# Where a weight tile begins: weights that meet 256 columns start 192 bytes into a tile 256 bytes longer

## The chip, the cores and the metric

The kernel runs on one core of one Trainium2 chip. The metric is the device time of one execution in microseconds. Three runs of the kernel before gave 2215.52, 2216.24 and 2218.65 us, a median of 2216.24.

## What is computed

A decoder trunk of two layers over 512 tokens of width 1024, in float32, batch 1. Each layer is: half a SwiGLU feed-forward block, a token mixer (retention in layer 0, forgetting attention in layer 1), half a SwiGLU again, and a gate that adds a projected per-layer input. Each has an RMSNorm ahead of it.

```python
def swiglu(x, w_in, w_out):
    g, u = jnp.split(x @ w_in, 2, axis=-1)
    return (jax.nn.silu(g) * u) @ w_out

for i in range(DEPTH):
    h = h + 0.5 * swiglu(rmsnorm(h, nw[0]), ffn_w_in[i, 0], ffn_w_out[i, 0])
    hn = rmsnorm(h, nw[1])
    h = h + (retention(hn, ...) if i % 2 == 0 else forgetting_attention(hn, ...))
    h = h + 0.5 * swiglu(rmsnorm(h, nw[2]), ffn_w_in[i, 1], ffn_w_out[i, 1])
    gate = jax.nn.sigmoid(rmsnorm(h, nw[3]) @ ple_w_gate[i])
    h = h + gate * (p[i] @ ple_w_proj[i])
```

The four feed-forward blocks (FFNs) have 2816 hidden columns each.

## The kernel before

**Products.** The activations stay in SBUF with the features on the partitions and the 512 tokens along the row. To keep float32 accuracy every operand is split into a high half (a rounding to the matmul's type, `fp32r`) and a low half (the rest), and a product is made as three: high by high, high by low, low by high. `mm3` (L311) does that with 512 columns of tokens, one moving operand of 128x512 each. The weights are the stationary operand, 128x128 a piece.

**The FFN's first matrix.** Each FFN has 22 column blocks of 128 hidden columns (gate and up). Two of them, the plain ones (`plain`, L511), are made in the ordinary way from products of 256 columns (L524): 8 steps over the width, two halves of the tokens, gate and up, three products each, 192 per FFN. The other 20 go through a scheme that saves products: the 2 by 2 blocks of the weights and of the activations are added up, and seven block products stand for eight (`start`, `one`, `two`, `three`, from L530). Each of the seven is a call of `product` (L490), whose matmuls are all on L493: 12 matmuls of 128x256, with the weight's high half 8 times and its low half 4. Of the seven, two take the block as it is loaded (`pair.t`, a tile that the profile calls `w`), four take sums of blocks (`pair.s`, tiles `s12` and `s34`, in the profile `s`), one takes the block `pair.x` (tile `a12`, in the profile `a`). So 84 products of 256 columns stand for a column block, 24 with `w`, 48 with `s`, 12 with `a`, and 4 x 20 x 84 = 6720 for all FFNs.

**Order in an FFN.** The hidden columns are worked in three chunks, (0, 6), (6, 14) and (14, 22), the first of which holds the two plain blocks. At the end of a chunk the next block is begun, and then `out_blocks` multiplies the chunk by the second matrix with `mm3`, 512 columns, from `w` tiles. So the 256-column stretch of the second and third chunk starts behind 512-column products. In the first chunk `two` copies a bank to SBUF with ScalarE (L545), behind the gating of the plain blocks, and `three` waits for it.

**Weights.** `Weights` holds a plan of all weight pieces in the order of their use. A piece (4 KB of each partition's row) is loaded from HBM into a `wraw` tile on SyncE's queue, ScalarE rounds it into the high half of a tile (L82, L121), and the low half is made by a subtraction on VectorE or GpSimd (L83), or by a negation and a transfer that adds the piece once more (L122, GpSimd's queue). `take` asks for two pieces beyond the one it returns. The high and low half lie one behind the other in a tile of 2 x 1024 floats, 8192 bytes of a row. Three such tiles rotate in the pool `wpool`. The last gating layer (`ple` with two parts of 256 tokens each) uses its last seven pieces for both parts: five in a pool `wkept` of the same kind of tile, two in `unit_b` tiles that are free by then. That layer's `mm3` products have 256 columns.

**Places.** The program puts its tiles one behind the other in each partition's row. Taken modulo 256 bytes, the activation tiles (`unit_a` to `unit_d`) begin at byte 32, and so does every 128x128 piece of the three rotating `w` tiles. Behind `wpool` lie the temporary tiles and the statistics, and then what a stage opens for itself: the FFN's `s12`, `s34` and `a12` tiles, or the five kept tiles, all of which begin at byte 224. The turned probabilities of the attention (`thi`, `tlo`) begin at byte 96. A step of a piece (512 bytes), of a half of the tokens (1024) or from the high to the low half does not change this remainder.

Of the kernel before, what the change touches and what calls it, by code (L numbers as in the profile page):

```python
# [12 lines left out]
F32R = mybir.dt.float32r  # L13
# [4 lines left out]
P = 128  # L18
# [17 lines left out]
class Pair:  # L36
# [3 lines left out]
    def __init__(self, ffn, q, r):  # L40
        self.ffn, self.q, self.r, self.direct = ffn, q, r, False
# [13 lines left out]
class Weights:  # L55
# [3 lines left out]
    def __init__(self, tc, raw_pool, pool):  # L59
        self.tc, self.nc, self.raw_pool, self.pool = tc, tc.nc, raw_pool, pool  # L60
        self.plan, self.ready, self.used = [], [], 0
        self.low = self.nc.vector
        self.limit, self.spare = None, []
        self.sum_pool, self.open_ffn, self.pairs_used = None, None, 0
        self.ahead, self.behind = 0, ()

    def emit(self, upto):
        while len(self.ready) < min(upto, self.limit):
            src = self.plan[len(self.ready)]
            self.ready.append(self.first(src) if isinstance(src, Pair) else self.chunk(src))  # L70
            self.emit_sums()

    def load(self, src):
        raw = self.raw_pool.tile([P, 1024], F32, name="wraw")
        self.nc.sync.dma_start(out=raw[:, : src.shape[1]], in_=src)
        return raw

    def split(self, raw, hi, lo, src=None):
        if self.low is None and src is not None:
            self.negated(raw, hi, lo, src)  # L80
            return
        self.nc.scalar.copy(hi, raw)  # L82
        self.low.tensor_tensor(out=lo, in0=raw, in1=hi.bitcast(F32), op=ALU.subtract)  # L83

    def chunk(self, src):
        n = src.shape[1]
        raw = self.load(src)
        if self.spare:
            tiles = [self.spare.pop(0)() for _ in range(4)]
            for i in range(2):  # L90
                self.split(raw[:, 512 * i : 512 * (i + 1)], tiles[i], tiles[2 + i])
            return Halves(tiles[0:2]), Halves(tiles[2:4])
        t = self.pool.tile([P, 2, 1024], F32R, name="w8")
        self.split(raw[:, :n], t[:, 0, :n], t[:, 1, :n], src)
        return t[:, 0, :], t[:, 1, :]

    def emit_parts(self, parts):

        nc = self.nc
        halves = lambda ap: ap.rearrange("p (h c) -> p h c", h=2)  # L100
        tiles = [
            (
                self.raw_pool.tile([P, 1024], F32, name="wraw"),
                self.pool.tile([P, 2, 1024], F32R, name="w8"),
            )
            for _ in range(2)
        ]
        for j0, j1 in parts:
            cs = slice(j0 * P, j1 * P)
            for src, (raw, t) in zip(self.plan, tiles):  # L110
                r, hi, lo = (halves(x)[:, :, cs] for x in (raw, t[:, 0, :], t[:, 1, :]))
                nc.sync.dma_start(out=r, in_=halves(src)[:, :, cs])
                nc.vector.tensor_copy(hi, r)
                nc.vector.tensor_tensor(out=lo, in0=r, in1=hi.bitcast(F32), op=ALU.subtract)
            yield
        self.ready += [(t[:, 0, :], t[:, 1, :]) for _, t in tiles]
# [7 lines left out]
    def first(self, pair):  # L124

        pair.raw = self.load(pair.q)
        pair.t = self.pool.tile([P, 2, 1024], F32R, name="w8")
        hi, lo = pair.t[:, 0, :], pair.t[:, 1, :]
        if pair.direct:
            self.split(pair.raw, hi, lo)  # L130
        else:
            self.negated(pair.raw, hi, lo, pair.q)
# [55 lines left out]
def trunk(ctx, tc, a):  # L188
# [16 lines left out]
    W = Weights(tc, wraw, wpool)  # L205
# [5 lines left out]
    ffn_src = []  # L211
    for i in range(4):
        ins = [Pair(i, a["ffn_w_in"][i, m, 0], a["ffn_w_in"][i, m, 1]) for m in range(NF)]
# [12 lines left out]
    ple_g = [[a["ple_gate"][l, m] for m in range(KB)] for l in range(2)]  # L226
    ple_p = [[a["ple_proj"][l, c] for c in range(2)] for l in range(2)]
# [11 lines left out]
    def plan_ple(l):  # L239
        W.plan += [ple_p[l][0]] + ple_g[l][0:5] + [ple_p[l][1]] + ple_g[l][5:8]  # L240
# [22 lines left out]
    plan_ffn(3)  # L263
    plan_ple(1)
    W.limit = len(W.plan) - KEPT


    hall = hpool.tile([P, KB, S], F32, name="hall")
# [42 lines left out]
    def mm3(out, wh, wl, xh, xl, first, last):  # L311
        nc.tensor.matmul(out, wh, xh, start=first, stop=False)  # L312
        nc.tensor.matmul(out, wh, xl, start=False, stop=False)  # L313
        nc.tensor.matmul(out, wl, xh, start=False, stop=last)  # L314
# [877 lines left out]
    norms[2].extra = ud  # L1192
    first = W.emit_parts(((0, 1), (1, 2), (2, 4)))
    next(first)
    load_x(1, 2)
    load_x(2, 4)
# [15 lines left out]
    def ffn_ple(i, l, n, mid, nxt, stack, apool, parts):  # L1212
        phi, plo = [], []

        def load():
            pv = a["pT"][l].rearrange("(b p) t -> b p t", p=P)
            for b in range(2):
                t1 = temp()
                nc.sync.dma_start(out=t1, in_=pv[b])
                phi.append(unit(uc))  # L1220
                plo.append(unit(uc))
                split(t1, phi[b], plo[b])

        ffn(i, n, mid, stack, apool, load)
        stack = open_ffn(i + 1) if i < 3 else None
        ple(l, mid, nxt, phi, plo, parts)
        return stack
# [101 lines left out]
```

## Time and profile before

| | before |
|---|---|
| median of three runs | 2216.24 us |
| the profiled execution | 2215.98 us |
| its span, first to last instruction | 2214.2 us |
| mean granted TensorE clock | 0.99 |
| TensorE matmuls | 13525 |
| VectorE, ScalarE, GpSimd busy | 66%, 54%, 21% |
| bytes read from HBM | 262.71 MB |

The profile is that of one execution. Times are in microseconds from the start of the span, and `ns` where it is said. PE is TensorE multiplying, PEld is TensorE loading weights, which overlaps with it, DVE is VectorE, ACT ScalarE, POOL GpSimd. A row names the line of the kernel, the engine, the operation, the tile that is written and those that are read (buffer numbers left out), and the shape. Matmuls overlap, so that the duration of one says less than the distance from the start of one to the start of the next. The timeline joins neighbours with the same line and tiles and gives the start of the group, its length and the count.

### The profile page before, as it was taken

To read this page: it belongs to the slowest core of one execution; us is meant where nothing else is said; L and a number is where in the kernel's file an instruction comes from. 1 tells how busy PE (TensorE), PEld (TensorE's weight loads), DVE (VectorE), ACT (ScalarE), POOL (GpSimd) and SP (SyncE) were. 2 spreads that over 40 slices of the span, in tenths; PEclk is the share of its full clock that TensorE was granted. 3 is DMA by queue.
4 is the path that set the end of the run, shared out by engine and by line. 5 is a ranking of instruction groups with operands and counts; after the bars stand their busy time and mean duration, and the time that the engine had idled before them with its cause. 6 is when DMAs were issued, how large, how long until landed. Compare 5 with 4: busy or idle time off the path is not lost.

```text
span 2214.2 us, 34442 instructions
## 1 busy us (share of the span) xinstructions
PE 2148.7 (97%) x13525; PEld 1933.3 (87%) x13525; DVE 1459.4 (66%) x2631; ACT 1203.1 (54%) x2027; POOL 466.8 (21%) x352
## 2 busy tenths in 40 slices
PE   7999999999999999999998999999999999999997
PEld 7999997888888798989887989898788898999987
DVE  8687776352533677867758677675575686777764
ACT  7565453343333564746545646364786775554643
POOL 0011013444344000101142001012243200110154
PEclk9999999999999999999999999999999999999999
DMA  5465562222222244645523456373622234655631
GB/s 174 111 168 150 141 163 95 74 94 81 94 78 86 77 126 128 167 126 149 144 92 97 117 142 178 117 166 102 154 86 86 77 112 113 162 155 142 156 105 39
DMA packets 85315, 267.08 MB, mean 121 GB/s; under 512 B 9360, under 2 KB 12944, under 8 KB 85152
## 3 DMA queue, kind: packets, MB, share of 16 engines
q1 hardware_dynamic: 63328, 209.78, 28.0%
q0 software_dynamic: 20592, 54.01, 14.4%
q8 instruction: 106, 1.74, 0.3%
q10 hardware_dynamic: 1232, 1.09, 0.1%
q14 instruction: 57, 0.47, 0.1%
HBM read 262.71 MB, written 2.13 MB: 120 GB/s over the span
## 4 chain that ended last, share of the span: by engine, by line
PE 81%; DVE 7%; ACT 5%; issue 4%; DMA 3%; POOL 1%; SPq 0%; DVEq 0%; ACTq 0%; POOLq 0%
PE bank L493 31%; PE bank L314 13%; PE bank L312 13%; PE bank L313 13%; PE bank L524 3%; DMA wraw<-in_ffn_w_in 2%; PE bank L678 2%; PE bank L679 2%; PE bank L680 2%; DVE w L83 1%; POOL w L83 1%; ACT p L982 1%; ACT w L82 1%; DVE sums L151 1%; DVE tlo L303 1%
## 5 line engine op out<-in xcount | busy, mean ns | idle before, releaser
L82 ACT CAST w<-wraw 128x1024 fp32r<-128x1024 f32 (+1 forms) x242 | 245.5, 1022 | 439.7 <-PE bank L314 257.3
L314 PE MATMUL bank<-unit_a,w 128*128 128x512 f32 x736 | 287.9, 391 | 4.3 <-DVE w L83 2.6
L312 PE MATMUL bank<-unit_a,w 128*128 128x512 f32 x736 | 289.2, 393 | 1.9 <-ACT w L82 1.6
L313 PE MATMUL bank<-unit_a,w 128*128 128x512 f32 x736 | 287.2, 390 | 0.2 <-DVE unit_a L303 0.2
L83 POOL TENSOR_TENSOR w<-wraw,w 128x1024 fp32r<-128x1024 f32 x93 | 226.5, 2439 | 273.7 <-ACT w L82 259.6
L314 PE MATMUL bank<-unit_d,w 128*128 128x512 f32 (+1 forms) x712 | 267.8, 376 | 4.7 <-DVE w L83 4.7
L312 PE MATMUL bank<-unit_d,w 128*128 128x512 f32 (+1 forms) x712 | 268.9, 378 | 3.3 <-ACT w L82 1.6
L82 ACT CAST s<-sums 128x512 fp32r<-128x512 f32 x320 | 191.1, 617 | 146.6 <-DVE sums L151 100.8
L313 PE MATMUL bank<-unit_d,w 128*128 128x512 f32 (+1 forms) x712 | 268.0, 376 | 1.7 <-DVE unit_d L303 1.7
L83 DVE TENSOR_TENSOR s<-sums,s 128x512 fp32r<-128x512 f32 x320 | 213.8, 686 | 83.1 <-ACT s L82 82.0
L122 POOL DMA_DIRECT2D a<-in_ffn_w_in x80 | 70.3, 878 | 654.4 <-ACT a L121 448.0
L83 DVE TENSOR_TENSOR w<-wraw,w 128x1024 fp32r<-128x1024 f32 (+1 forms) x149 | 175.8, 1185 | 23.4 <-ACT w L82 23.3
L493 PE MATMUL bank<-unit_b,s 128*128 128x256 f32 x880 | 185.4, 277 | 0.0
L493 PE MATMUL bank<-unit_d,s 128*128 128x256 f32 x1140 | 178.3, 276 | 0.0
L493 PE MATMUL bank<-unit_a,s 128*128 128x256 f32 x1260 | 176.1, 277 | 1.9 <-ACT unit_a L376 1.1
L585 DVE SCALAR_TENSOR_TENSOR tmp<-bank,rows 128x512 f32<-128x512 f32 x96 | 66.1, 690 | 166.3 <-PE bank L314 165.1
L314 PEld LDWEIGHTS bank<-unit_a,w 128*128 128x128 f32 x736 | 138.5, 188 | 35.7 <-DVE w L83 4.4
L312 PEld LDWEIGHTS bank<-unit_a,w 128*128 128x128 f32 x736 | 138.6, 188 | 32.3 <-ACT w L82 3.5
L313 PEld LDWEIGHTS bank<-unit_a,w 128*128 128x128 f32 x736 | 138.7, 188 | 28.7 <-DVE unit_a L303 0.5
L493 PEld LDWEIGHTS bank<-unit_a,s 128*128 128x128 f32 x1260 | 158.8, 188 | 2.7 <-ACT unit_a L376 1.6
L314 PEld LDWEIGHTS bank<-unit_d,w 128*128 128x128 f32 x712 | 134.1, 188 | 30.8 <-DVE w L83 6.6
L312 PEld LDWEIGHTS bank<-unit_d,w 128*128 128x128 f32 x712 | 134.1, 188 | 30.1 <-ACT w L82 3.3
(268 smaller groups left out, 4780.1 us busy)
## 6 DMA issues: line engine op xcount, KB each, us to landing
wraw<-in_ffn_w_in SPq DMA_DIRECT2D x174, 512.0 KB, 4.3
wraw<-in_ffn_w_out SPq DMA_DIRECT2D x64, 512.0 KB, 4.7
w<-in_ffn_w_in POOLq DMA_DIRECT2D x56, 512.0 KB, 5.3
a<-in_ffn_w_in POOLq DMA_DIRECT2D x80, 256.0 KB, 6.2
wraw<-in_ffn_w_out SPq DMA_DIRECT2D x32, 384.0 KB, 3.5
wraw<-in_ret_qk SPq DMA_DIRECT2D x16, 512.0 KB, 3.5
wraw<-in_ret_v SPq DMA_DIRECT2D x16, 512.0 KB, 3.6
wraw<-in_ret_g SPq DMA_DIRECT2D x16, 512.0 KB, 3.4
```

The source lines that it names most:

```text
L82: self.nc.scalar.copy(hi, raw)
L83: self.low.tensor_tensor(out=lo, in0=raw, in1=hi.bitcast(F32), op=ALU.subtract)
L122: self.nc.gpsimd.dma_start(out=lo, in_=src, accum_op=ALU.add)
L312: nc.tensor.matmul(out, wh, xh, start=first, stop=False)
L313: nc.tensor.matmul(out, wh, xl, start=False, stop=False)
L314: nc.tensor.matmul(out, wl, xh, start=False, stop=last)
L493: add = lambda w, x, start, stop: nc.tensor.matmul(out, w, x, start=start, stop=stop, skip_group_check=True)
L524: nc.tensor.matmul(o[:, HALVES[t]], x[:, ks], y, start=k == t == q == 0, stop=k == KB - 1 and q == 2, skip_group_check=True,)
L585: nc.vector.scalar_tensor_tensor(out=t1, in0=o, scalar=-0.5, in1=n.r, op0=ALU.mult, op1=ALU.mult)
L678: nc.tensor.matmul(os[t], xh, wh[:, js], start=k == 0, stop=False)
L679: nc.tensor.matmul(os[t], xh, wl[:, js], start=False, stop=False)
L680: nc.tensor.matmul(os[t], xl, wh[:, js], start=False, stop=k == KB - 1)
```

## The change

Every weight tile becomes 2112 floats long, 8448 bytes in place of 8192. A new helper, `wide`, takes the tile and gives back the 2 x 1024 floats in it that are used. For a piece in the set `narrow` they begin at float 48, byte 192; for all others at byte 0, and the spare bytes stand behind them. `narrow` holds the pieces of the first matrices of all four FFNs (`pair.q` and `pair.r`) and all gate and projection pieces of the last gating layer. These are the pieces whose products have 256 columns. The pieces of retention, attention, the second matrices and the first gating layer meet 512 columns and begin at byte 0.

```diff
+        self.narrow = set()
...
+    def wide(self, src):
+
+        at = 48 if id(src) in self.narrow else 0
+        t = self.pool.tile([P, 2112], F32R, name="w8")
+        return t[:, at : at + 2048].rearrange("p (a c) -> p a c", a=2)
...
-        t = self.pool.tile([P, 2, 1024], F32R, name="w8")
+        t = self.wide(src)
         self.split(raw[:, :n], t[:, 0, :n], t[:, 1, :n], src)
...
-                self.pool.tile([P, 2, 1024], F32R, name="w8"),
+                self.wide(src),
             )
-            for _ in range(2)
+            for src in self.plan[:2]
...
-        pair.t = self.pool.tile([P, 2, 1024], F32R, name="w8")
+        pair.t = self.wide(pair.q)
...
+    for ins, _ in ffn_src:
+        W.narrow |= {id(x) for pair in ins for x in (pair.q, pair.r)}
+    W.narrow |= {id(x) for x in ple_g[1] + ple_p[1]}
```

The instructions of all five engines stand in the same order as before, word for word, and wait for the same things. What changes is addresses. In the three rotating tiles the narrow pieces come to byte 224 modulo 256, and the others stay at byte 32. In the five kept tiles the pieces come from byte 224 to byte 160. All tiles behind `wpool` move by 768 bytes, which leaves them where they were modulo 256.

## The prediction

> **What bounds the kernel now.** I read the page first: who is busy, and who is on the chain that ended last.
>
> ```profile
> span 2214.2 us, 34442 instructions
> ...
> PE 2148.7 (97%) x13525; PEld 1933.3 (87%) x13525; DVE 1459.4 (66%) x2631; ACT 1203.1 (54%) x2027; POOL 466.8 (21%) x352
> ...
> PE 81%; DVE 7%; ACT 5%; issue 4%; DMA 3%; POOL 1%; SPq 0%; DVEq 0%; ACTq 0%; POOLq 0%
> ```
>
> TensorE is the bound, and the rest feeds it. Since busy matmuls overlap, 97% does not say how fast one follows another. So next come the rows of the line that multiplies halves (L493, all 256 columns), minimum/median/maximum of one instruction:
>
> ```profile
> L493 PE MATMUL bank<-unit_d,s x1140: 276/276/278, 1222.6 to 2093.6; 128*128 128x256 f32 x190
> L493 PEld LDWEIGHTS bank<-unit_d,w x540: 187/192/192, 1221.3 to 2090.8; 128*128 128x128 f32 x180
> L493 PE MATMUL bank<-unit_d,w x540: 278/283/283, 1221.4 to 2090.9; 128*128 128x256 f32 x180
> L493 PE MATMUL bank<-unit_d,a x240: 276/276/278, 1236.2 to 2095.0; 128*128 128x256 f32 x120
> ```
>
> The same shape with the same moving tiles takes 276 ns with weights from `s` or `a` and 283 from `w`. What one product really costs is the distance from start to start, which the timeline gives (start, length of the group, group and count):
>
> ```profile
> 126.66 0.39 PE L314 MATMUL bank<-unit_d,w 128*128 128x512 f32 x1
> 126.88 0.88 PE L493 MATMUL bank<-unit_b,w 128*128 128x256 f32 x6
> ...
> 128.32 2.88 PE L493 MATMUL bank<-unit_a,s 128*128 128x256 f32 x24
> 131.04 1.60 PE L493 MATMUL bank<-unit_a,w 128*128 128x256 f32 x12
> 132.48 0.73 PE L493 MATMUL bank<-unit_b,s 128*128 128x256 f32 x5
> ...
> 135.20 0.73 PE L493 MATMUL bank<-unit_b,a 128*128 128x256 f32 x5
> ...
> 136.56 0.88 PE L493 MATMUL bank<-unit_b,w 128*128 128x256 f32 x6
> ```
>
> 24 products with `s` take 131.04 - 128.32 = 2.72 us, 113.3 ns each; 12 with `w` 132.48 - 131.04 = 1.44 us, 120.0 each; 12 with `a` (135.20 to 136.56) 113.3. No wait stands between them. So a product with `w` costs 6.7 ns more than its neighbours, at full clock and without a gap.
>
> What differs is the place. The moving units all start at byte 32 of a stretch of 256 (their addresses modulo 256), `w` too; `s` and `a` start at byte 224, 192 further on. That it is the place and not the tile's name, the last gating layer shows, where weights lie in `w` and `unit_b` at byte 32 and in kept `w` tiles at byte 224:
>
> ```profile
> 2153.17 0.28 PE L312 MATMUL bank<-unit_d,unit_b 128*128 128x256 f32 x1
> ...
> 2154.61 0.28 PE L312 MATMUL bank<-unit_d,unit_b 128*128 128x256 f32 x1
> ...
> 2186.43 0.28 PE L312 MATMUL bank<-unit_d,w 128*128 128x256 f32 x1
> ...
> 2188.81 0.28 PE L312 MATMUL bank<-unit_c,w 128*128 128x256 f32 x1
> ...
> 2190.28 0.28 PE L312 MATMUL bank<-unit_d,w 128*128 128x256 f32 x1
> ...
> 2192.40 0.28 PE L312 MATMUL bank<-unit_d,w 128*128 128x256 f32 x1
> ```
>
> At byte 32: 12 products in 1.44 us, 120.0 each. At byte 224: 21 products in 2.38 us, 113.3 each, from a `w` tile. But the last pair of rows, byte 224 again, has 18 products in 2.12 us, 117.8 each. The same place has two paces. That is the weak point of this forecast, and it comes back below.
>
> **The change part by part.** No instruction is added, removed or moved on any engine; only addresses change. First, the 2832 products of 256 columns with weights at byte 32 of the three rotating tiles get them at byte 224: in the four FFNs 24 of the 84 products of each of 20 column blocks, 1920 at L493; the two plain blocks, 192 per FFN, 768 at L524; and 144 in the last gating layer.
>
> L493: 1920 x (120.0 - 113.3) = 12.8 us. Some 50 of them run at cold clock and gain nothing, so I take 12.3. This lies on TensorE's own path, with no cover to lose. L524: 768 x 6.7 = 5.1 us at most. Two of these four stretches open with waits for weights:
>
> ```profile
> PE bank L493 <- ACT tmp L545: 14.2, 6, 5.5
> ...
> PE bank L524 <- ACT w L82: 5.7, 1, 5.7
> ...
> PE bank L524 <- POOL w L83: 2.4, 1, 2.4
> ```
>
> What TensorE gains ahead of such a wait, the wait gives back, for it ends when the cast is done; I take 3 us. The wait at L545 (a copy that ScalarE does behind the plain blocks' gating) has only 12 products with `w` close ahead of it in each FFN, 4 x 12 x 6.7 ns = 0.3 us, to be taken off. The gating layer: 144 x between 2.2 (117.8) and 6.7 ns is 0.3 to 1.0 us; 240 products in the kept tiles go from byte 224 to 160, where no row stands; at 113.3 to 120.0 for 117.8 that is -1.1 to +0.5 us. Together 0.
>
> Second, all else behind the longer tiles moves by 768 bytes, three times 256: modulo 256 nothing changes for `s`, `a` and the statistics, and I take 0 (the third rival prices it). The products of 512 columns keep byte 32:
>
> ```profile
> 1605.49 0.39 PE L314 MATMUL bank<-unit_d,w 128*128 128x512 f32 x1
> ...
> 1609.57 0.39 PE L314 MATMUL bank<-unit_d,w 128*128 128x512 f32 x1
> ...
> 1615.23 0.40 PE L1012 MATMUL bank<-thi,unit_b 128*128 128x512 f32 x1
> 1615.47 0.40 PE L1013 MATMUL bank<-tlo,unit_b 128*128 128x512 f32 x1
> 1615.71 0.34 PE L1012 MATMUL bank<-thi,unit_b 128*128 128x384 f32 x1
> ```
>
> 18 of them in 4.08 us are 226.7 ns each, twice 113.3: they pay nothing now. The two behind them, whose weights lie 192 bytes past the moving tile modulo 256 (32 against 96), take 240.
>
> Third, casts, subtractions and transfers write 192 bytes further on. The one hint that this could matter are the transfers that add onto the low half:
>
> ```profile
> w<-in_ffn_w_in POOLq DMA_DIRECT2D x56, 512.0 KB, 5.3
> a<-in_ffn_w_in POOLq DMA_DIRECT2D x80, 256.0 KB, 6.2
> ```
>
> Those into `a`, at byte 224, land later with half the bytes. A block of 84 products takes about 9.7 us (126.88 to 136.56), and weights are asked for two chunks ahead, which hides a microsecond; with that cover gone it would be 56 x 0.9 = 50 us, but nothing waits for them in the FFNs today. I take 0.
>
> Fourth, the pace. A stretch at byte 32 seems to bring what follows into the fast pace. Behind a wait in the second FFN the granted clock (PEclk) is at half, and then back:
>
> ```profile
> 815.00:818.00 3.00, 3.00 (x16) 3.00 (x16) 1.26 (x3) 1.98 (x4) 0.00 (x0) 0.50 0.00 0
> 819.00:822.00 3.00, 3.00 (x28) 3.00 (x27) 2.56 (x4) 1.69 (x4) 0.85 (x1) 1.00 0.50 72
> ```
>
> ```profile
> 814.10 0.50 PE L493 MATMUL bank<-unit_b,w 128*128 128x256 f32 x2 [2.28 <-ACT tmp L545]
> ...
> 821.38 0.65 PE L493 MATMUL bank<-unit_b,w 128*128 128x256 f32 x4
> ...
> 822.83 0.40 PE L493 MATMUL bank<-unit_b,s 128*128 128x256 f32 x2
> ...
> 825.65 0.40 PE L493 MATMUL bank<-unit_b,w 128*128 128x256 f32 x2
> ...
> 827.08 0.39 PE L493 MATMUL bank<-unit_b,s 128*128 128x256 f32 x2
> ...
> 829.80 0.39 PE L493 MATMUL bank<-unit_b,a 128*128 128x256 f32 x2
> ```
>
> With the clock back, the 24 products with `s` from 822.83 still take 2.82 us, 117.5 each; then 12 with `w`; the next 24 with `s` take 2.72 us, 113.3. With no more byte-32 runs inside a chunk, a chunk that starts in the slow pace stays there. Each FFN's first chunk of 4 blocks, 336 products, starts behind the wait at L545, as above. In the slow pace its 240 `s` and `a` products lose 4.2 ns each and its 96 with `w` gain 2.5 and not 6.7: 1.0 + 0.4 = 1.4 us per FFN, 5.6 in all. I take half, 2.8. The other two chunks of 8 blocks start out of 512-column products, which run without loss, and there I take the fast pace.
>
> Sum: -12.3 - 3.0 + 0.3 + 2.8 = -12.2 us. The profiled execution took 2215.98 us, within 0.3 of the median 2216.24, so 2203.8; I say 2204.
>
> On the floor of 113.3: by the Trainium skill, "TensorE: Matmul & The Clock Gate", section "Back-to-back issue gap", an isolated product of N columns costs N / 2.4 + 2.5 ns, 109 for 256. By that an estimate of the L493 gain would be 1920 x 10.9 = 21 us; the trace has no long run of this shape under 113.3, and the measurement decides.
>
> **The rivals.** *The slow pace everywhere* (the other side). Place: the second and third chunks of each FFN. Mechanism: coming out of 512-column products the first weights at byte 224 cost the moving stream something, as at 1615.23, and no byte-32 run ever ends it. Price: 4800 products with `s` and `a` x (117.5 - 113.3) = +20.2 us, and `w` gains only (1920 + 500) x 2.5 = 6.1: +14, 2230 us. With only the first chunks fast it is about +10. It decides when 45% of the products run slow: fast, a product gains 6.7 x 24/84 = 1.9 ns on average; slow, it loses 4.2 x 60/84 - 2.5 x 24/84 = 2.3. For it: 1615.23 and 2190.28. Against it: today the runs with `s`, entered from `w`, sit at 113.3 in all but a few places, and 512-column products and 113.3 are the same rate per column.
>
> *Nothing changes*: the place is not the cause, or what TensorE saves is handed back in waits for ScalarE. Against it stand the rows at 2186.43. 2216 us. The Trainium skill, "SBUF — State Buffer", section "Who interferes with whom", gives TensorE two independent read ports, one for each operand, and says that it never waits on anyone; by that rule a start address cannot matter, and the trace, 120.0 against 113.3, disagrees.
>
> *The stretch is longer than 256 bytes.* Then `s` and `a`, which move by 768 bytes, change place modulo 512, and one of the three rotating tiles stands half a stretch off. No long run shows such a place. Bounds: `s` and `a` between 113.3 and 120.0, up to 4800 x 6.7 = +32 us, less the gain above: 2204 to 2236.
>
> **How the numbers follow.** Forecast 0.52, its own range 2199 (all in the fast pace: 12.3 + 4.5 us) to 2208. Slow pace 0.30, 2225 to 2231. Nothing 0.10, 2213 to 2218. Longer stretch 0.08. A measurement here can tell about 0.2%, 4.4 us, from no change. Faster: 0.52 and 0.03 of the last, 0.55; within 0.2% 0.10; slower 0.30 and 0.05, 0.35. The range 2199 to 2231 holds the first three cases and leaves out the far end of the last.
>
> **What would show it.** Right: at L493 `w` at 276 like `s`; in the third chunk 24 `s` in 2.72 us and then 12 `w` in 1.36; the 512-column products at 226.7. First-chunk doubt: `s` at 2.82 us per 24 behind the wait at L545 alone. Wrong: `s` rows with a median of 279 or 280 in the later chunks (slow pace), `w` still at 283 (nothing), or `s` off both paces (longer stretch); longer waits for casts or for the adding transfers would speak for the third edit.

## The result, and the profile after

| | before | after |
|---|---|---|
| median | 2215.99 us (7 runs) | 2229.19 us (7 runs, 2221.72 to 2233.68) |
| ratio, 95% interval | | 1.0057, 1.0037 to 1.0077 |
| the profiled execution | 2215.98 us | 2221.72 us |

The kernel became slower by 0.57%, where 0.5% faster was forecast. What came about is the first rival, the slow pace everywhere, which had been priced at 2230 us.

The page of the changed kernel, in the lines that were shown of before (the line numbers are 10 higher now: products on L503, plain blocks on L534, the wait for `tmp` on L555):

```profile
span 2219.9 us, 34442 instructions
...
PE 2155.4 (97%) x13525; PEld 1940.6 (87%) x13525; DVE 1458.1 (66%) x2631; ACT 1202.8 (54%) x2027; POOL 465.8 (21%) x352
...
PE 81%; DVE 7%; ACT 5%; issue 4%; DMA 2%; POOL 1%; SPq 0%; DVEq 0%; ACTq 0%; POOLq 0%
```

TensorE has the same number of matmuls and is busy for 6.7 us more; the other engines do what they did. The rows of the line that multiplies halves (minimum/median/maximum of one instruction in ns) say which products it is:

```profile
L503 PE MATMUL bank<-unit_d,s x1140: 276/279/280, 1222.6 to 2099.4; 128*128 128x256 f32 x190
L503 PEld LDWEIGHTS bank<-unit_d,w x540: 187/188/188, 1221.3 to 2096.5; 128*128 128x128 f32 x180
L503 PE MATMUL bank<-unit_d,w x540: 276/279/280, 1221.4 to 2096.6; 128*128 128x256 f32 x180
L503 PE MATMUL bank<-unit_d,a x240: 276/279/280, 1236.1 to 2100.9; 128*128 128x256 f32 x120
```

`w` went from a median of 283 to 279, but `s` and `a`, whose place modulo 256 did not change, from 276 to 279. The timeline shows the pace at the entry to the second chunk, the place at which before had runs of 113.3 and 120.0 (start, length of the group, group and count):

```profile
126.22 0.39 PE L324 MATMUL bank<-unit_d,w 128*128 128x512 f32 x1
126.45 0.87 PE L503 MATMUL bank<-unit_b,w 128*128 128x256 f32 x6
...
127.86 2.99 PE L503 MATMUL bank<-unit_a,s 128*128 128x256 f32 x24
130.69 1.58 PE L503 MATMUL bank<-unit_a,w 128*128 128x256 f32 x12
132.10 0.75 PE L503 MATMUL bank<-unit_b,s 128*128 128x256 f32 x5
...
134.93 0.75 PE L503 MATMUL bank<-unit_b,a 128*128 128x256 f32 x5
...
136.34 0.87 PE L503 MATMUL bank<-unit_b,w 128*128 128x256 f32 x6
...
205.59 0.40 PE L322 MATMUL bank<-unit_d,w 128*128 128x512 f32 x1
```

Twelve `w` take 127.86 - 126.45 = 1.41 us, 117.5 each; 24 `s` 2.83 us, 117.9; 12 `w` 1.41; 12 `a` 1.41. All three kinds go at one pace of 117.8 ns, from the first product behind the 512-column ones to the last of the chunk. The 672 products of this chunk take 205.59 - 126.45 = 79.14 us. Before, they end here:

```profile
204.32 0.40 PE L312 MATMUL bank<-unit_d,w 128*128 128x512 f32 x1
```

That is 204.32 - 126.88 = 77.44 us, 1.70 less. The other second chunks differ by the same, and the third ones (636 products; 73.27 before and 74.90 after where no wait falls into them) by 1.63: 4 x (1.70 + 1.63) = 13.3 us. The medians differ by 13.2 us, and the interval of the ratio reaches from 8 to 17, so these eight chunks can carry all of it.

The two profiled executions differ by less, 5.7 us. Their granted clock fits that (span and mean clock, first of before, then of after):

```profile
core 0: 2214.2 us, clock 0.990
```

```profile
core 0: 2219.9 us, clock 0.993
```

The execution of after had 0.003 more clock, which is worth about 0.003 x 2214 = 6.6 us. One such place is the wait in the second FFN, where before had a clock of 0.50 from 815 to 818. In the view by stretches (length, busy PE, clock, DMA) after has its full clock there:

```profile
812.00:818.00 6.00, 3.98 (x33) 1.00 0.25 88
```

It was the fastest of its seven runs, so the medians are the better comparison here.

### The profile page after: what moved, and what is told of

The parts are those of the page before. It is cut to its first block, busy times and chain, and to the rows that moved or that the text cites. A ratio compares the mean times of both kernels' runs of the same rounds, so it can differ in the third digit from the quotient of the medians.

```text
span 2219.9 us, 34442 instructions
## 1 busy us (share of the span) xinstructions
PE 2155.4 (97%) x13525; PEld 1940.6 (87%) x13525; DVE 1458.1 (66%) x2631; ACT 1202.8 (54%) x2027; POOL 465.8 (21%) x352
## 4 chain that ended last, share of the span: by engine, by line
PE 81%; DVE 7%; ACT 5%; issue 4%; DMA 2%; POOL 1%; SPq 0%; DVEq 0%; ACTq 0%; POOLq 0%
PE bank L503 34%; PE bank L324 13%; PE bank L322 13%; PE bank L323 13%; PE bank L534 3%; PE bank L688 2%; PE bank L689 2%; PE bank L690 2%; DVE w L90 1%; POOL w L90 1%; ACT p L992 1%; DMA wraw<-in_ffn_w_in 1%; ACT w L89 1%; ACT p L994 1%; DVE tlo L313 1%
## 5 line engine op out<-in xcount | busy, mean ns | idle before, releaser
L503 PE MATMUL bank<-unit_b,s 128*128 128x256 f32 x880 | 188.1, 280 | 0.0
L503 PE MATMUL bank<-unit_d,s 128*128 128x256 f32 x1140 | 182.9, 279 | 0.0
L503 PE MATMUL bank<-unit_a,s 128*128 128x256 f32 x1260 | 181.0, 280 | 1.8 <-ACT unit_a L386 1.1
L503 PEld LDWEIGHTS bank<-unit_a,s 128*128 128x128 f32 x1260 | 162.6, 188 | 2.6 <-ACT unit_a L386 1.6
```

Source lines behind the costliest of these rows:

```text
L503: add = lambda w, x, start, stop: nc.tensor.matmul(out, w, x, start=start, stop=stop, skip_group_check=True)
```

## The experiments

The theory after the result: the pace depends on how a stretch is entered; only a run of weights at another place brings the products back to 113.3 ns; with all weights at byte 224 no such run is left. The rivals: the shift by 768 bytes did it (another place modulo 512), or longer tiles cost something in themselves. In what follows "chunk" alone is a second or third chunk, a place is a byte modulo 256, and a pace is the distance from start to start, counted from all starts in the trace. The two times given are medians, of the run and of before in the same session; the ratio is taken from all runs of both and can differ from the quotient of the medians by about 0.1%.

**1. The longer tiles alone.** The changed kernel with all pieces at byte 0 of their tiles, which is place 32 again:

```diff
-        at = 48 if id(src) in self.narrow else 0
+        at = 0
```

> The tiles 256 bytes longer, every piece at byte 0 of its tile: what is left of the change is that all tiles behind them move by 768 bytes. Entry theory (a stretch at byte 224 falls into the slow pace of 117.8 ns where it is entered from 512-column products or a wait, and only a run of weights at byte 32 brings the fast pace of 113.3 back): nothing moves modulo 256, so s and a stay at 113.3 ns, w at 120.0, and the time is that of before, 2216 us within 5. Theory of the longer stretch (places count modulo 512, and s and a are slow at 480): s and a at 117.5 to 117.8 here too, +20 to +22 us, 2236 to 2238.

Measured: 2216.87 us against 2218.95, ratio 1.0001 (0.9987 to 1.0015).

```profile
L503 PE MATMUL bank<-unit_d,s x1140: 276/276/415, 1223.6 to 2101.6; 128*128 128x256 f32 x190
L503 PE MATMUL bank<-unit_d,w x540: 274/283/415, 1222.4 to 2098.9; 128*128 128x256 f32 x180
```

`s` at 276 and `w` at 283, as before the change. Neither the longer tiles nor the shift by 768 bytes cost anything that shows within 0.15%; the 192 bytes do.

**2. The 192 bytes with `s` and `a` back in their old place modulo 512.** Tiles of 2176 floats:

```diff
-        t = self.pool.tile([P, 2112], F32R, name="w8")
+        t = self.pool.tile([P, 2176], F32R, name="w8")
```

> As the changed kernel, with tiles 512 bytes longer in place of 256, so that s and a come back to byte 224 modulo 512 and every narrow piece lies at 224 modulo 512. Entry theory: the slow pace as in the changed kernel, s, a and w at 117.8 ns, 2222 to 2232 us. Longer stretch: s, a and w all at 113.3 ns, 2199 to 2204 us.

Measured: 2231.59 us against 2218.95, ratio 1.0068 (1.0048 to 1.0087); `s`, `a` and `w` at 117.8 in all chunks, as in the changed kernel:

```profile
L503 PE MATMUL bank<-unit_d,s x1140: 277/279/415, 1227.8 to 2108.5; 128*128 128x256 f32 x190
```

A stretch of 512 bytes has no part in it.

**3. Blocks 2, 6 and 14 back at byte 32.** These were meant to be the first behind the 512-column products or the wait:

```diff
+        W.narrow -= {id(ins[m].q) for m in (2, 6, 14)}
```

> As the changed kernel, but the loaded piece of the column blocks 2, 6 and 14 of each FFN, the first that stands behind the 512-column products or the wait of a chunk, is at byte 0. Entry theory: these 24 products of a chunk run at 120.0 and all that follows, w at byte 224 with it, at 113.3; 4 x 17 x 24 = 1632 products gain 6.7 ns, 10.9 us, and the plain blocks up to 3: 2202 to 2207 us. In the second FFN's first chunk, which comes out of a halved clock, the slow pace may stay. Longer stretch: s and a stay at 117.8, 2222 to 2232 us.

Measured: 2214.62 us against 2218.95, ratio 0.9993 (0.9977 to 1.0008). A miss: 2202 to 2207 was expected. The entry to the second chunk shows that blocks 6 and 14 were not the first:

```profile
126.86 0.87 PE L504 MATMUL bank<-unit_b,w 128*128 128x256 f32 x6
...
128.27 2.99 PE L504 MATMUL bank<-unit_a,s 128*128 128x256 f32 x24
131.09 1.59 PE L504 MATMUL bank<-unit_a,w 128*128 128x256 f32 x12
132.53 0.73 PE L504 MATMUL bank<-unit_b,s 128*128 128x256 f32 x5
...
135.25 0.73 PE L504 MATMUL bank<-unit_b,a 128*128 128x256 f32 x5
...
136.60 0.62 PE L504 MATMUL bank<-unit_b,w 128*128 128x256 f32 x4
```

The first block behind the 512-column products is number 7, not 6: `one` and `two` of the next block are done ahead of `three` of the last one. So the chunk enters at byte 224, and its first 36 products run at 117.8 (24 `s` from 128.27 to 131.09 in 2.82 us). Then `three` of block 6 comes with 12 `w` at byte 32 (1.44 us, 120.0), and behind them `s` takes 135.25 - 132.53 = 2.72 us, 113.3, and stays there to the end of the chunk. This one row is the turn from one pace to the other. The late turn costs little: the second chunks take 76.47 us, 0.96 less than before. What is missing of the gain lies elsewhere. The first chunks came out of their waits at 117.8 and stayed there, and three of the four third chunks fell back to 117.8 in their last third (73.4, 73.6 and 74.1 us, against 72.3 in the fourth).

**4. The right blocks.** Blocks 7 and 15 behind the 512-column products, and 3 and 4 behind the wait:

```diff
+        W.narrow -= {id(ins[m].q) for m in (3, 4, 7, 15)}
```

> The changed kernel, but the weights `w` of blocks 3, 4, 7 and 15 of each FFN stay at byte 32: blocks 7 and 15 are the first that TensorE meets behind the 512-column products, 3 and 4 the first behind the wait for `tmp`. Theory (a run at byte 32 sets the fast pace, and what enters at byte 224 from elsewhere goes on at 117.8): `s` and `a` at 113.3 ns from the first run on in all second and third chunks, `w` at 113.3 in all blocks but these; a chunk of 672 products in 672 x 113.3 ns + 24 x 6.7 ns = 76.3 us (77.43 before, 79.14 with the change), one of 636 in 72.2 (73.3 and 74.9); eight of them 9 us under before; with the plain blocks' 1 to 2 us some 2205 to 2210 where before takes 2216 to 2219. Rival (the place of `w` next to `s` decides, block by block, and not what ran before it): 117.8 again in all blocks whose `w` is at byte 224, 2226 to 2230.

Measured: 2214.29 us against 2217.47, ratio 0.9984 (0.9975 to 0.9994). The second chunks came out as expected: 76.31 us each, `s` and `a` at 113.3 from the first run on. The time is a miss (2205 to 2210 was expected), for the third chunks did not keep the pace. The timeline of the first FFN:

```profile
296.19 2.88 PE L504 MATMUL bank<-unit_a,s 128*128 128x256 f32 x24
301.08 2.93 PE L504 MATMUL bank<-unit_a,w 128*128 128x256 f32 x12 [2.01 <-ACT tmp L556]
303.81 1.04 PE L504 MATMUL bank<-unit_b,s 128*128 128x256 f32 x5
...
305.51 1.57 PE L504 MATMUL bank<-unit_a,s 128*128 128x256 f32 x12
306.92 0.75 PE L504 MATMUL bank<-unit_b,a 128*128 128x256 f32 x5
...
308.33 0.87 PE L504 MATMUL bank<-unit_b,w 128*128 128x256 f32 x6
```

Up to 298 us the pace is 113.3. TensorE then waits 2.01 us for ScalarE's copy, starts again at half clock (12 `w` in 2.73 us), and when the clock is back it runs at 117.8 (12 `a` in 1.41 us) until the chunk ends: only byte 224 is left there to run from. So a wait, too, can throw a stretch into the slow pace. The half clock is not needed for it: in the other three FFNs the third chunk turns slow behind waits of 0.8, 0.5 and 1.4 us at full clock. In the four third chunks some 170 of 636 products run slow in this way, 170 x 4.5 ns = 0.8 us each. That does not explain all: the profiled execution took 2207.43 us, inside what was expected, but it was the lowest of ten, and what the median lost beside it stays open.

**5. The low half alone moved.** The high half of each narrow piece at byte 32, the low half at 224, so that each run with `w` has 8 products of the one and 4 of the other:

```diff
-        at = 48 if id(src) in self.narrow else 0
-        t = self.pool.tile([P, 2112], F32R, name="w8")
-        return t[:, at : at + 2048].rearrange("p (a c) -> p a c", a=2)
+        half = 1072 if id(src) in self.narrow else 1024
+        t = self.pool.tile([P, 2176], F32R, name="w8")
+        return t[:, : 2 * half].rearrange("p (a c) -> p a c", a=2)[:, :, :1024]
```

> Of every narrow piece the high half at byte 0 and only the low half 192 bytes on (tiles 512 bytes longer). Entry theory: the 8 high products of each w product bring the fast pace in at 120.0, the 4 low ones and then s and a run at 113.3: 160 x 4 x 6.7 ns = 4.3 us less, 2210 to 2214 us; in the plain blocks high and low alternate, which no row shows. Longer stretch: the same for the FFN products, so this run does not tell the two apart; it asks whether 8 products at byte 32 are enough.

Measured: 2212.84 us against 2218.95, ratio 0.9976 (0.9962 to 0.9991), as expected. In the chunks 8 of 12 products with `w` take 120.0 and 4 take 113.3 ns, and `s` and `a` 113.3 throughout: with products at byte 32 in every run of `w`, those at byte 224 bring their whole gain.

**6. Everything at byte 32.** The kernel before, with 64 bytes ahead of each FFN's own tiles:

```diff
         stack = ExitStack()
+        pad = stack.enter_context(tc.tile_pool(name=f"pad{i}", bufs=1))
+        nc.vector.memset(pad.tile([P, 16], F32, name="pad"), 0.0)
```

> The kernel before, with 64 bytes of padding ahead of each FFN's own tiles, so that `s` and `a` begin at byte 32 modulo 256 like `w` and like the moving tiles. Theory (the weights' place alone sets the 120.0): every product of 256 columns in the chunks 120.0 ns, 4800 x 6.7 ns = 32 us more, 2248 to 2251. Rival (it is `w` itself, whose tiles rotate through three places or are written by another engine): `s` and `a` stay at 113.3, within 0.2% of before.

Measured: 2244.14 us against 2217.47, ratio 1.0121 (1.0094 to 1.0148).

```profile
L495 PE MATMUL bank<-unit_d,s x1140: 279/283/415, 1235.4 to 2125.8; 128*128 128x256 f32 x190
L495 PE MATMUL bank<-unit_d,w x540: 278/283/415, 1234.2 to 2122.9; 128*128 128x256 f32 x180
```

`s` now has the 283 of `w`, and every run in the chunks 120.0. So the 120.0 belongs to the place and to no tile, as the prediction took it. The medians differ by 26.7 us and not by 32. The four runs lie between 2238 and 2248 us; the profiled one, 2248.27, is one of the two long ones, and only these two reach what was expected.

**7. `w` at byte 96.** The changed kernel with 64 bytes in place of 192:

```diff
-        at = 48 if id(src) in self.narrow else 0
+        at = 16 if id(src) in self.narrow else 0
```

> The changed kernel with the narrow weights 64 bytes into their tile instead of 192: `w` at byte 96 modulo 256, `s` and `a` at 224 as before. Theory (only weights in the very place of the moving tile, byte 32, cost 120.0, and only what enters at byte 224 turns slow): `w` at or near 113.3, and as each chunk enters with `w`, `s` and `a` at 113.3 too: 12 to 15 us less than before, 2202 to 2207. Rival (any entry that isn't at byte 32 leads to the slow pace): `s` and `a` at 117.8, 2226 to 2232. Rival (the loss falls off with distance): `w` between 113.3 and 120.0, time between 2204 and 2217.

Measured: 2208.34 us against 2217.47, ratio 0.9960 (0.9944 to 0.9976).

```profile
125.80 0.87 PE L503 MATMUL bank<-unit_b,w 128*128 128x256 f32 x6
...
127.22 2.99 PE L503 MATMUL bank<-unit_a,s 128*128 128x256 f32 x24
130.04 1.52 PE L503 MATMUL bank<-unit_a,w 128*128 128x256 f32 x12
131.40 0.73 PE L503 MATMUL bank<-unit_b,s 128*128 128x256 f32 x5
...
134.12 0.73 PE L503 MATMUL bank<-unit_b,a 128*128 128x256 f32 x5
...
135.48 0.84 PE L503 MATMUL bank<-unit_b,w 128*128 128x256 f32 x6
```

The chunk enters in the slow pace even here (12 `w` in 1.42 us, 24 `s` in 2.82). But the next run with `w`, the step from byte 224 back to 96, takes 1.36 us, 113.3 each, and from then on everything does. The median is 1.3 us above what the first theory expected, and the way to it was another: byte 96 at the entry did not save the first runs. Note that the step from 96 to 224, at 127.22, changed nothing; the step back from 224 to 96, at 130.04, did.

**8. `w` at byte 160.** The same with 128 bytes:

```diff
-        at = 48 if id(src) in self.narrow else 0
+        at = 32 if id(src) in self.narrow else 0
```

> The changed kernel with the narrow weights 128 bytes into their tile: `w` at byte 160 modulo 256, `s` and `a` at 224. The same theories as for 64 bytes: 113.3 for all, 2202 to 2207, if only byte 224 at the entry turns slow; `s` and `a` at 117.8, 2226 to 2232, if any entry but byte 32 does; if byte 160 is itself like 224, `w` at 117.8 as well.

Measured: 2232.66 us against 2217.47, ratio 1.0066 (1.0043 to 1.0089), near what was expected for any entry but byte 32. In the chunks `w` takes 119.0 ns on average (most single ones between 115 and 124) and `s` and `a` 117.8. Steps between 160 and 224 never bring the fast pace.

**9. All at byte 96.** The kernel of experiment 7 with 128 bytes ahead of each FFN's own tiles, so that `s` and `a` are at 96 as well:

```diff
         stack = ExitStack()
+        pad = stack.enter_context(tc.tile_pool(name=f"pad{i}", bufs=1))
+        nc.vector.memset(pad.tile([P, 32], F32, name="pad"), 0.0)
```

> The changed kernel with the narrow weights 64 bytes in, and 128 bytes of padding ahead of each FFN's own tiles: `w`, `s` and `a` all at byte 96 modulo 256, so that inside a chunk the weights' place no longer changes. Theory A (a change of place brings the loads back into step; without one a chunk stays in the pace in which it begins): the second and third chunks at 117.8 ns throughout, as with all three at byte 224, 2226 to 2232. Theory B (byte 96 is a good place by itself, only 224 and 160 turn slow): 113.3 behind the first few products, 2203 to 2209.

Measured: 2223.61 us against 2216.50, ratio 1.0029 (1.0013 to 1.0046), a little below what theory A expected.

```profile
128.21 0.87 PE L505 MATMUL bank<-unit_b,w 128*128 128x256 f32 x6
...
129.62 2.99 PE L505 MATMUL bank<-unit_a,s 128*128 128x256 f32 x24
132.45 1.58 PE L505 MATMUL bank<-unit_a,w 128*128 128x256 f32 x12
133.86 0.75 PE L505 MATMUL bank<-unit_b,s 128*128 128x256 f32 x5
...
136.69 0.75 PE L505 MATMUL bank<-unit_b,a 128*128 128x256 f32 x5
...
138.10 0.87 PE L505 MATMUL bank<-unit_b,w 128*128 128x256 f32 x6
```

24 `s` in 2.83 us, 12 `w` in 1.41, 24 `s` in 2.83, and so on through each second chunk. The same place that ran at 113.3 beside byte 224 runs at 117.8 alone. For a stretch entered from 512-column products theory A holds: without a change of place it stays slow. But a wait can bring the fast pace without one. The first chunks come out of their wait at 113.3 in three FFNs of four, and two third chunks turn fast behind waits of 0.13 and 0.93 us at full clock: about 3 x 1.4 + 2 x 0.8 = 5.8 us against a slow pace throughout.

**10. Mirrored.** `w` stays at byte 224, as in the changed kernel, and the padding of experiment 9 puts `s` and `a` at 96:

> The kernel with 64 bytes mirrored: `w` stays at byte 224 modulo 256 as in the changed kernel, and 128 bytes of padding put `s` and `a` at 96. Theory A (any change of place inside a block, between two places that are each able to run at 113.3, brings a chunk into the fast pace within its first blocks): `w`, `s` and `a` at 113.3 behind the first few dozen products, eight chunks in 76.3 or 72.2 us, 2205 to 2210. Rival (it is the step from 224 to 96 at the start of a run with `w` that does it, since `w` stands ahead of each pair of runs with `s`): another pattern, with `s` or `a` runs in the slow pace at places, between 2210 and 2230.

Measured: 2207.50 us against 2216.38, ratio 0.9960 (0.9946 to 0.9975).

```profile
124.16 0.87 PE L505 MATMUL bank<-unit_b,w 128*128 128x256 f32 x6
...
125.57 2.90 PE L505 MATMUL bank<-unit_a,s 128*128 128x256 f32 x24
128.31 1.52 PE L505 MATMUL bank<-unit_a,w 128*128 128x256 f32 x12
129.67 0.73 PE L505 MATMUL bank<-unit_b,s 128*128 128x256 f32 x5
```

The first 12 `w` take 1.41 us; with the first step to byte 96 the 24 `s` take 2.74, and from 128.31 on all is at 113.3. So the turn does not need a run of `w`. But it is again the step from 224 to 96 that makes it, as in experiment 7, and the direction of the step does matter: in the traces of experiments 7, 10 and 11, counted at full clock and with no wait at the step, a step from 224 to 96 out of the slow pace led to 113.3 in 44 of 49 cases, a step from 96 to 224 in none of 24. Theory A, for which any change would do, is too wide. Against the changed kernel only 128 bytes ahead of `s` and `a` are new, and the time falls from 0.6% above before to 0.4% below it.

**11. Byte 96 in the kept tiles too.** The kernel of experiment 7, with 128 bytes in the tiles of the last gating layer:

```diff
-        at = 16 if id(src) in self.narrow else 0
+        at = self.at if id(src) in self.narrow else 0
...
+                W.at = 32
                 W.spare = [lambda: unit(ub)] * 8
```

(`self.at` starts at 16.)

> The changed kernel with the narrow weights 64 bytes into their rotating tile and, in the five tiles that are kept for the last gating layer, 128 bytes in: `w` at byte 96 modulo 256 everywhere, `s` and `a` at 224. All theories: the FFNs as with 64 bytes, 9 to 12 us under before (the time of the kernel with 64 bytes was 2208.3 against 2217.5). The kept tiles go from byte 32 to 96: if weights in the moving tile's place cost 6.7 ns there too, 240 x 6.7 ns = 1.6 us less than with 64 bytes, about 2206; otherwise the same as with 64 bytes.

Measured: 2207.10 us against 2216.50, ratio 0.9949 (0.9935 to 0.9964). It is the lowest ratio of all, but its interval overlaps with those of experiments 7 and 10. The products with weights in the five kept and the rotating tiles of the gating layer, 384 in all, took 48.4 us, each from its start to the next one, against 49.6 in experiment 7 and before. That is 1.2 of the expected 1.6 us.

The second chunks by place, with the moving tiles always at byte 32 (the ratio is that of the whole kernel):

| byte of `w` / of `s` and `a` (modulo 256) | `w`, ns | `s` and `a`, ns | ratio |
|---|---|---|---|
| 32 / 224 (before) | 120.0 | 113.3 | 1 |
| 32 and 224 / 224 | 117.7 | 113.3 | 0.9976 |
| 224 / 224 (after) | 117.8 | 117.8 | 1.0057 |
| 96 / 96 | 117.8 | 117.8 | 1.0029 |
| 32 / 32 | 120.0 | 120.0 | 1.0121 |
| 160 / 224 | 119.0 | 117.8 | 1.0066 |
| 96 / 224 | 113.3 behind the first 12 | 113.3 behind the first 24 | 0.9960 |
| 224 / 96 | 113.3 behind the first 12 | 113.3 | 0.9960 |

## Why the prediction was wrong

**The step that failed** stands in "Fourth, the pace": the second and third chunks "start out of 512-column products, which run without loss, and there I take the fast pace". They enter at 117.8, with weights at byte 224 (changed kernel) and at byte 96 (experiments 7 and 9), and in the changed kernel they stay there to the end. For these eight chunks the sum had a gain of 1488 x 6.7 ns = 10.0 us by their `w`; what came is the loss of 13.3 us. The text had the means to see it: it had noted that in before a run at byte 32 brings the fast pace, and that the change takes away all such runs; it applied this to the first chunks and not to the others. In before every chunk entered with `w` at byte 32, so that no row of it showed an entry at 224 behind 512-column products. That "against" of the rival, runs with `s` at 113.3 all through the chunks, rested on the very runs that the change removed.

**Where the 120.0 comes from** was right: it is the place (experiment 6), and weights at byte 224 or 96 can run at 113.3 (experiments 5, 7, 10). The gain exists where the fast pace is kept: in experiment 7 three of the four second chunks take 76.32 us against 77.43, 1.1 us less with 192 products of `w`, where 6.7 ns each make 1.3. The median is 9.1 us under before, and the plain blocks have 2.7 of that (116.2 us from start to start before, 113.5 in experiment 7).

**L534**, the plain blocks, forecast at -3.0 us: 116.2 us became 115.1, -1.1, each product counted from its start to the next one, waits included. They run at 117.8 and not at 113.3; 768 x (120.0 - 117.8) is 1.7, and the waits take some of it back. The gating layer, forecast at 0, has 49.6 us in both.

**The wait at L545** (now L555) was to grow by 0.3 us. It has no sign of that in the profiled execution, where it is shorter than the 14.2 us of before:

```profile
PE bank L503 <- ACT tmp L555: 12.4, 5, 5.5
...
PE bank L534 <- ACT w L89: 5.7, 1, 5.7
...
PE bank L534 <- POOL w L90: 2.4, 1, 2.4
```

But this row adds up two things. The waits in the third chunks come and go from one execution to the next: in experiment 1, at the paces of before, the same row has 17.9 us. In the four first chunks alone the wait is 12.5 us before, 11.9 in the changed kernel and 13.0 in experiment 7. There the slower products leave ScalarE more time, and the faster ones less. So with the fast pace it grows by 0.5 us. The thought of the prediction was right and its 0.3 somewhat low: it counted 12 products with `w` ahead of the wait, and there are 24 behind the plain blocks (the first `one` and the next).

**First chunks, 2.8 us:** behind the wait three of the four ran slow and one fast, 3 x 1.4 = 4.2 us of the 5.6. That half came near it was luck; nothing in before told how many would.

**The shift, the writes and the transfers at 0** were right: experiment 1 for the shift; the transfers that add onto the low half land after 5.4 us (5.3 before), and nothing in the FFNs waits for them:

```profile
w<-in_ffn_w_in POOLq DMA_DIRECT2D x56, 512.0 KB, 5.4
a<-in_ffn_w_in POOLq DMA_DIRECT2D x80, 256.0 KB, 6.2
```

**The rival's price** was 2230 and its mechanism the one that was found, but for its cause: it put the slow entry down to the first weights at byte 224. Byte 96 enters just as slowly.

**Nothing changes**, the second rival, is out: the rows of the table above differ, with 113.3, 117.8 and 120.0. By the Trainium skill, "SBUF — State Buffer", section "Who interferes with whom", TensorE reads its two operands through ports of their own and waits on nobody. As the prediction read that rule, all rows would be alike.

**What stays open:** why there are two paces at one place, and why steps from 224 to 96 and from 32 to 224 bring the fast one back while those from 96 to 224 and between 160 and 224 do not. No run here took the loading of the weights and the reading of the moving tile apart. And no run moved the moving tiles of the chunks: whether it is the distance from them that counts, or the place of the weights itself, is not shown.

## What to carry to other kernels

When a profile shows a fast and a slow row for one shape, look for what brings the fast one about before moving the slow one to the same place: here the "bad" place was also what reset the good one. In a kernel like this one, put the weights of alternating runs into two places of a 256-byte stretch that are both free of the moving tile's own, and not all into one. The pair that worked here is 96 and 224 beside a moving tile at 32; 160 and 224 did not. And an entry, behind other shapes, waits or a drop of the clock, has to be read from rows of its own.

## What the runs showed of the hardware

- The start of the weights modulo 256 bytes changes the pace of 128x256 `fp32r` products behind one another. With the moving tile at byte 32 it is 120.0 ns for weights at byte 32 too, 113.3 or 117.8 at bytes 96 and 224, and 119.0 on average at byte 160 beside runs at 224.
- The pace has a memory. Entered from 512-column products with all weights at byte 224, or all at 96, a chunk of 672 products stays at 117.8 ns from first to last (79.14 us). A step from 224 to 96 mostly brought 113.3 (in 44 of 49 cases, and the chunk then takes 76.3 us), one from 96 to 224 did in none of 24. A run at byte 32 mostly does, at once or the second time: in before 12 of them leave the 24 `s` from 822.83 at 117.5, and the next 12 bring 113.3.
- A wait draws anew, with or without a drop of the clock. In the changed kernel three first chunks came out of it at 117.8 and one at 113.3, of which only the first chunk of the first FFN had the clock at half. In experiment 4 all four third chunks went from 113.3 to 117.8, and in experiment 9, with all weights at byte 96, two third chunks went from 117.8 to 113.3.
